# Moving part of the sums of squares at the end of the SwiGLUs to GpSimd, and spreading norm factors by fp32 products

## The chip, the cores and the metric

The kernel runs on one core of a Trainium2 chip. The metric is the device time of one execution in microseconds (us), as the median of several runs. Engines are named as in the profile: PE (TensorE, matrix products; PEld are its weight loads), DVE (VectorE), ACT (ScalarE), POOL (GpSimd), SP (SyncE, which issues DMAs). SBUF is the on-chip memory, PSUM the banks into which PE writes.

## What is computed

One inference step of a trunk of two layers, width 1024, for a prompt of 1024 tokens and for 8 x 4 sample tokens that share the weights. Layer 0 mixes tokens by sliding-window attention with sinks, layer 1 by a gated recurrence. What bears on the change are the norms and the SwiGLUs:

```
def rms_norm(x, g):
    y = xf * lax.rsqrt(jnp.mean(xf * xf, axis=-1, keepdims=True) + EPS)
    return (y * g.astype(jnp.float32)).astype(x.dtype)

def swiglu(h, w_in, w_out):
    g, u = jnp.split(h @ w_in, 2, axis=-1)
    return (jax.nn.silu(g) * u) @ w_out

for layer in range(DEPTH):
    x = x + mixer(rms_norm(x, ...))        # attention, then recurrence
    x = x + swiglu(rms_norm(x, ffn_norm[layer]), w_ffn_in[layer], w_ffn_out[layer])
y = rms_norm(x, final_norm)
```

The mean of a norm runs over the 1024 features of a token, so each of the five norms needs, per token, a sum of squares, a power of -1/2 of it, and a product of x with the result and with the norm's weight.

## The kernel before

**Layout.** Features lie on the 128 partitions, in 8 blocks (index m or kb), tokens along the free dimension in three column groups t = 0, 1, 2 of 384, 384 and 288 columns (the last: 256 prompt and 32 sample tokens). Every large product is made as three fp32r products of high and low parts (`mm3`, L313): high times high, high times low, low times high. A tile is split into such parts by `split`: ScalarE copies the high part (L351), VectorE subtracts it for the low one (L352). Weights are split on their way in: ScalarE copies (L84), VectorE subtracts (L88).

**Phases.** Attention, first FFN (l = 0), recurrence, second FFN (l = 1), final norm. In an FFN most of the products over pairs of hidden blocks are made in units of seven products instead of eight (`second`, `unit`); what is left goes through `h_out`, which ends the FFN.

**The end of an FFN (`h_out`).** For each t, and in it for each m of 8: six products into a PSUM bank, on VectorE the sum with x (L1029, with high priority), on ScalarE the square of the new x (L368), on VectorE the sum of the squares `acc` (L369). The square of m = 0 is written to `acc` itself (L365). The squares lie in a ring of two buffers that other temporary tiles share (tag "xs"). In the first FFN the squares of t = 2 are made only after `h_out`.

**A norm (`rms`, `spread`).** Three fp32 products of one column, blocks of `acc` times ones (L376), give the sums, one token per partition; VectorE scales and adds epsilon (L381), GpSimd raises to -1/2 (L382), VectorE takes the high part (L383, CAST) and the low part (L384). Six fp32r products, the high and low column of each of three token blocks times the identity `idr` (L395, L396), spread the factors over all partitions in a PSUM bank, from which ScalarE copies them (L402, `rs`). Then x is multiplied: in the mixers' and FFNs' norms at L428, after which `split` follows; in the final norm on VectorE at L1391 from the PSUM bank, and for two m of t = 1 and of t = 2 on GpSimd at L1389 (table `POOLED`). There are five norms in three groups, 15 passes in all.

**Order.** PE and SP execute in the order in which the code calls them; so where `rms` and `spread` stand between groups of products is written by hand, by `steps` in `second`: n0 and n1 are the norms of t = 0 and t = 1 that follow the FFN.

```
steps = [{}, {2: n0[1:2], 5: n0[3:4]}, {1: n1[1:2], 4: n1[3:4]}]
```

That is: the sum of t = 0 after m = 2 of t = 1, its spread after m = 5; those of t = 1 after m = 1 and m = 4 of t = 2. The order on VectorE, ScalarE and GpSimd is set by a scheduler, from its own costs and from priorities (`high_priority`). Each of these engines works strictly in its order.

**In attention** the lines that the prediction touches are: L706 and L707, the exponential of the sample tokens on ScalarE; L610 and L612, the prompt's; L712 to L714, the sample's division on VectorE, whose result `ss` PE transposes at L719; `pr`, the split probabilities; and L769, the sum of the attention's output with x. L428 there is the norm ahead of the first FFN.

Of the kernel before, what the change touches and what calls it, by code (L numbers as in the profile page):

```python
# [39 lines left out]
NSH = 4  # L40
POOLED = [(), (5, 7), (2, 5)]

# [210 lines left out]
class Kern:  # L253
# [103 lines left out]

    def square(self, t, kb):
        nc = self.nc
        W = WID[t]  # L360
        if t not in self.acc:
            self.acc[t] = self.gt.tile([P, WMAX], F32, name=self.nm("acc"), tag="acc", bufs=2)
            if W < WMAX:
                nc.gpsimd.memset(self.acc[t][:, W:WMAX], 0.0)
            nc.scalar.activation(self.acc[t][:, :W], self.xview(t, kb), AF.Square)  # L365
        else:
            sq = self.gt.tile([P, WMAX], F32, name=self.nm("sq"), tag="xs", bufs=2)
            nc.scalar.activation(sq[:, :W], self.xview(t, kb), AF.Square)  # L368
            nc.vector.tensor_tensor(self.acc[t][:, :W], self.acc[t][:, :W], sq[:, :W], OP.add)  # L369

    def rms(self, t):
        nc = self.nc
        mm = nc.tensor.matmul
        ps = self.bank()
        for b in range(3):
            mm(ps[:, WMAX + b:WMAX + b + 1], self.acc[t][:, b * P:(b + 1) * P], self.ones[:, 0:1], start=True, stop=True)  # L376
        del self.acc[t]
        col = self.gt.tile([P, 2, 3], F32, name=self.nm("rc"), tag="rc", bufs=2)
        hl = self.gt.tile([P, 2, 3], F32R, name=self.nm("rh"), tag="rh", bufs=2)
        with self.tc.high_priority(PRI):  # L380
            nc.vector.tensor_scalar(col[:, 0, :], ps[:, WMAX:WMAX + 3], 1.0 / D, EPS, op0=OP.mult, op1=OP.add)  # L381
            nc.gpsimd.tensor_tensor(col[:, 1, :], col[:, 0, :], self.mhalf, OP.pow)  # L382
            nc.vector.tensor_copy(hl[:, 0, :], col[:, 1, :])  # L383
            nc.vector.tensor_tensor(hl[:, 1, :], col[:, 1, :], hl[:, 0, :].bitcast(F32), OP.subtract)  # L384
        self.hl[t], self.col[t] = hl, col

    def spread(self, t, direct):
        nc = self.nc
        W = WID[t]
        mm = nc.tensor.matmul  # L390
        hl = self.hl[t]
        ps = self.bank()
        for b in range(3):
            o, n = b * P, min(P, W - b * P)
            mm(ps[:, o:o + n], hl[:, 0, b:b + 1].to_broadcast([P, P]), self.idr[:, :n], start=True, stop=False)  # L395
            mm(ps[:, o:o + n], hl[:, 1, b:b + 1].to_broadcast([P, P]), self.idr[:, :n], start=False, stop=True)  # L396
        self.rp[t] = ps
        if direct:
            self.rs[t] = ps
            return  # L400
        rs = self.gt.tile([P, WMAX], F32, name=self.nm("rs"), tag="rs", bufs=2)
        nc.scalar.activation(rs[:, :W], ps[:, :W], AF.Copy)  # L402
        self.rs[t] = rs
# [370 lines left out]
    def attn_phase(self):  # L774
# [31 lines left out]
        def head():  # L806
            nc.sync.dma_start(self.ident, self.I["ident"])
            nc.sync.dma_start(self.vec[:, KB:], self.I["vec"][:, KB:])
            nc.gpsimd.tensor_copy(self.idr, self.ident)

# [32 lines left out]
    def ffn_phase(self, l, before, after):  # L843
# [105 lines left out]
        def sums(j):  # L949
# [10 lines left out]
            if j == 3:  # L960
                self.freeall(self.xt[0] + self.xt[1])

        def reload(i):
            for t in range(NT):
                if i == 0:
                    self.xt[t] = []
                self.xt[t].append(self.act_tile([P, 4, WMAX], F32, "x"))
                nc.sync.dma_start(self.xt[t][i][0][:, :, :WID[t]], self.xd[t][:, 4 * i:4 * i + 4, :])
# [50 lines left out]
        def h_out(w0, w1, h, t, steps):  # L1019
            W = WID[t]  # L1020
            ws = (w0, w1)
            for m in range(KB):
# [7 lines left out]
                if l == 1 or t < 2:  # L1030
                    with tc.high_priority(PRI if t == 2 else 0):
                        self.square(t, m)
                for fn in steps.get(m, ()):
# [58 lines left out]
        def second():  # L1092
# [17 lines left out]
            def pin(on):  # L1110
# [4 lines left out]
                    [lambda: fetch(0, 3, 9), lambda: reload(1)], [lambda: do(1, "parts"), lambda: do(2, "load")],  # L1115
                    [lambda: pin(True)], [lambda: pin(False)]]
            items = []
# [16 lines left out]
            w = [x.w for x in M[n:]]  # L1134
            steps = [{}, {2: n0[1:2], 5: n0[3:4]}, {1: n1[1:2], 4: n1[3:4]}]
            last = [Item(lambda a, b, h, t=t: h_out(a, b, h, t, steps[t]), w + [H[t]],
# [19 lines left out]
        L += lead[6] + p[:2] + n0[4:] + [p[2]] + n1[4:]  # L1156
        if l == 0:
            L += [lambda m=m: self.square(2, m) for m in range(KB)]
        return L, leave
# [245 lines left out]
    def run(self):  # L1405
        nc, tc = self.nc, self.tc
        with tc.tile_pool(name="const", bufs=1) as cp, tc.tile_pool(name="g", bufs=1) as self.gp, \
# [6 lines left out]
            self.early = []  # L1414
            self.pinned = False
            self.xt, self.xn, self.acc, self.rs, self.q, self.att, self.hl, self.rp, self.col = {}, {}, {}, {}, {}, {}, {}, {}, {}
            self.ones = cp.tile([P, P], F32, name="ones")
# [4 lines left out]
            self.ident = cp.tile([P, P], F32, name="ident")  # L1422
            self.idr = cp.tile([P, P], F32R, name="idr")
            n2, n1, n3 = self.norm_steps(2, "ffn0"), self.norm_steps(1, "ffn1"), self.norm_steps(2, "ffn1")
# [109 lines left out]
```

## Time and profile before

| | |
|---|---|
| median of 3 runs | 2188.36 us (2187.37 to 2188.39) |
| the profiled execution | 2189.78 us |
| its span, first to last instruction | 2187.9 us |
| mean granted clock of PE in it | 0.987 |
| PE busy | 2129.7 us, 97% |
| VectorE, ScalarE, GpSimd busy | 1493.8, 1005.4, 232.8 us |
| sums of squares on VectorE (L369) | 105 x 525 ns = 55.1 us |
| factor's high and low part (L383, L384) | 15 x 169 and 15 x 158 ns |
| spread, high and low (L395, L396) | 45 x 271 and 45 x 293 ns |

The tables of the profile are read so: a line names an engine, the operation with what it writes and reads (`out<-in`, buffer numbers left out), partitions x elements, and how often; then the busy time, the mean of one, and the idle time of the engine just before it with what ended that. A timeline has the start, the time that it took and, in brackets, the idle time ahead and what ended it. A table of windows has, for each stretch, its length, the busy time of PE, PEld, DVE, ACT and POOL with the number of instructions, the granted clock of PE, the DMAs' share and GB/s. Matmuls are pipelined, so that the durations of single ones overlap.

### The profile page before, as it was taken

Reading aid. Unit: us, or ns where it says so; the run is one execution under the profiler, and the core shown is the slowest. Engines: PE = TensorE matmul, PEld = TensorE weight load, DVE = VectorE, ACT = ScalarE, POOL = GpSimd, SP = SyncE. Lnnn points to the kernel's source line nnn. Section 1 sums busy time; section 2 is a strip of 40 time slices with the busy share of each in tenths; the row PEclk is TensorE's granted clock in tenths of the full one; section 3 lists DMA queues with packets and bytes.
Section 4 is the critical chain, followed back from the end, with each engine's and each line's share of the span. In section 5 each row is a group of like instructions: output and inputs, shape, how many; then the busy total and the mean of one; then the engine's idle time right before and its main releaser. Section 6 shows DMA issues by size and latency. Waiting matters only on the chain.

```text
span 2187.9 us, 35226 instructions
## 1 busy us (share of the span) xinstructions
PE 2129.7 (97%) x13608; PEld 2104.4 (96%) x13608; DVE 1493.8 (68%) x2940; ACT 1005.4 (46%) x1835; POOL 232.8 (11%) x322
## 2 busy tenths in 40 slices
PE   9999999999999998999999989999999999989997
PEld 8899989999999998999999989999999999979997
DVE  6877787756656664666786787787666656556667
ACT  5666665434444443212268887754444444321122
POOL 1223230000000001232100000000000000112321
PEclk9999999999999999999999999999999999999998
DMA  5332434333343338765212123442343343676632
GB/s 193 101 104 79 129 110 159 112 106 132 104 160 120 118 137 321 287 226 185 93 43 64 59 80 114 153 147 77 137 135 129 107 162 129 220 295 220 221 121 80
DMA packets 131632, 310.12 MB, mean 142 GB/s; under 512 B 14152, under 2 KB 84872, under 8 KB 131464
## 3 DMA queue, kind: packets, MB, share of 16 engines
q1 hardware_dynamic: 130128, 306.95, 40.7%
q8 instruction: 107, 1.75, 0.3%
q10 hardware_dynamic: 1336, 0.92, 0.1%
q14 instruction: 61, 0.50, 0.1%
HBM read 223.15 MB, written 86.65 MB: 142 GB/s over the span
## 4 chain that ended last, share of the span: by engine, by line
PE 84%; DVE 7%; ACT 4%; DMA 3%; issue 1%; POOL 0%; SPq 0%; ACTq 0%; DVEq 0%; POOLq 0%
PE mm L313 80%; DVE w L88 1%; PE pt L633 1%; DMA o<-od 1%; ACT w L84 1%; DMA od<-hi 1%; PE s L585 1%; DVE s L603 1%; ACT s L610 1%; DVE xn L352 0%; DVE acc L369 0%; PE mm L376 0%; DVE pr L352 0%; DMA raw<-in_wz 0%; ACT g L1252 0%
## 5 line engine op out<-in xcount | busy, mean ns | idle before, releaser
L313 PE MATMUL mm<-xn,w 128*128 128x384 f32 (+1 forms) x5808 | 927.3, 317 | 10.6 <-DVE w L88 3.8
L313 PEld LDWEIGHTS mm<-xn,w 128*128 128x128 f32 x5808 | 901.5, 188 | 16.5 <-DVE w L88 4.5
L313 PE MATMUL mm<-o,w 128*128 128x384 f32 (+1 forms) x2928 | 478.4, 325 | 19.8 <-DVE x L1017 19.8
L313 PEld LDWEIGHTS mm<-o,w 128*128 128x128 f32 x2928 | 475.2, 191 | 20.9 <-DVE x L1017 20.9
L313 PE MATMUL mm<-T,w 128*128 128x384 f32 x1920 | 351.4, 338 | 0.9 <-ACT sg L986 0.9
L313 PEld LDWEIGHTS mm<-T,w 128*128 128x128 f32 x1920 | 338.8, 188 | 1.4 <-ACT sg L986 1.4
L88 DVE TENSOR_TENSOR w<-raw,w 128x1024 fp32r<-128x1024 f32 x202 | 245.3, 1222 | 111.2 <-ACT w L84 110.7
L1017 DVE TENSOR_TENSOR x<-mm,x 128x384 f32<-128x384 f32 x360 | 191.1, 534 | 141.3 <-PE mm L313 140.2
L84 ACT ACTIVATE w<-raw 128x1024 fp32r<-128x1024 f32 x204 | 215.1, 1056 | 129.4 <-PE mm L313 61.9
L135 ACT ACTIVATE w<-raw 128x1024 fp32r<-128x1024 f32 x84 | 85.3, 1053 | 328.4 <-POOL raw L159 296.2
L156 POOL TENSOR_TENSOR raw<-raw 128x256 f32<-128x256 f32 x40 | 29.6, 739 | 1191.4 <-DVE w L136 1191.4
L136 DVE TENSOR_TENSOR w<-raw,w 128x1024 fp32r<-128x1024 f32 x84 | 102.7, 1222 | 15.4 <-ACT w L135 15.4
L625 POOL TENSOR_SCALAR s<-s,sm 128x256 f32<-128x256 f32 (+1 forms) x128 | 83.9, 672 | 208.2 <-DVE sm L623 97.5
L313 PE MATMUL mm<-att,w 128*128 128x384 f32 (+1 forms) x576 | 97.1, 324 | 0.0
L313 PE MATMUL mm<-y,w 128*128 128x384 f32 (+1 forms) x576 | 93.5, 322 | 0.0
L313 PEld LDWEIGHTS mm<-att,w 128*128 128x128 f32 x576 | 91.3, 188 | 1.9
L313 PEld LDWEIGHTS mm<-y,w 128*128 128x128 f32 x576 | 92.4, 188 | 0.0
L610 ACT ACTIVATE s<-s,sm 128x256 f32<-128x256 f32 (+1 forms) x128 | 61.7, 483 | 45.8 <-DVE sm L607 45.7
L894 ACT ACTIVATE hi<-e 128x384 fp32r<-128x384 f32 x80 | 41.8, 523 | 88.6 <-DVE e L1008 33.4
L117 DVE TENSOR_TENSOR w<-raw,w 128x1024 fp32r<-128x1024 f32 x40 | 48.9, 1223 | 36.5 <-ACT w L115 36.4
L368 ACT ACTIVATE sq<-x 128x384 f32<-128x384 f32 (+1 forms) x105 | 50.9, 492 | 41.6 <-DVE x L1029 20.4
L992 DVE TENSOR_TENSOR sg<-mm,sg 128x384 f32<-128x384 f32 x40 | 22.2, 555 | 62.0 <-PE mm L313 62.0
(208 smaller groups left out, 2286.9 us busy)
## 6 DMA issues: line engine op xcount, KB each, us to landing
o<-od SPq DMA_DIRECT2D x70, 768.0 KB, 7.0
od<-hi SPq DMA_DIRECT2D x140, 192.0 KB, 2.0
raw<-in_wg SPq DMA_DIRECT2D x44, 512.0 KB, 4.0
raw<-in_wu SPq DMA_DIRECT2D x44, 512.0 KB, 4.5
raw<-in_wz SPq DMA_DIRECT2D x40, 512.0 KB, 3.7
od<-e SPq DMA_DIRECT2D x80, 192.0 KB, 2.0
raw<-in_wq SPq DMA_DIRECT2D x24, 512.0 KB, 3.5
raw<-in_wo SPq DMA_DIRECT2D x24, 512.0 KB, 3.6
```

Source lines behind the costliest of these rows:

```text
L84: nc.scalar.activation(self.t[:, 0, :], raw, AF.Copy)
L88: nc.vector.tensor_tensor(self.t[:, 1, :], raw, self.t[:, 0, :].bitcast(F32), OP.subtract)
L117: tt(d[:, 1, :], g, d[:, 0, :].bitcast(F32), OP.subtract)
L135: pin(nc.scalar.activation(self.t[:, 0, :], raw, AF.Copy))
L136: pin(nc.vector.tensor_tensor(self.t[:, 1, :], raw, self.t[:, 0, :].bitcast(F32), OP.subtract))
L156: tt(d, c, d, OP.add)
L313: mm = lambda *a, **k: self.nc.tensor.matmul(*a, skip_group_check=more, **k)
L368: nc.scalar.activation(sq[:, :W], self.xview(t, kb), AF.Square)
L610: nc.scalar.activation(s[:, j, :N], s[:, j, :N], AF.Exp, bias=sm[:, 1, j:j + 1], accum_out=sm[:, 3, j:j + 1])
L625: nc.gpsimd.tensor_scalar(s[:, j, :N], s[:, j, :N], sm[:, 4, j:j + 1], 1.0, op0=OP.mult, op1=OP.mult)
L894: nc.scalar.activation(hi.bitcast(F32R), src, AF.Copy)
L1017: tc.keep_in_program_order(tt(x, ps[:, :WID[t]], x, OP.add))
```

## The change

1. `square` can send its add to GpSimd. A table `SQUARES` says which: in the first FFN the squares 1 to 7 of t = 0; in the second those, 4 to 6 of t = 1, and 1 to 4 of t = 2. That is 21 of the 105 adds.
2. The squares of `h_out` lie in a ring of four buffers in a free activation slot, which the ring takes ahead of `h_out` and, in the first FFN, gives back before the squares of t = 2.
3. A spread is three fp32 products with the fp32 identity instead of six fp32r ones. The high and low parts of the factor (L383, L384) go, and `idr` with the cast that made it.
4. The sum and spread of t = 1 stand after m = 3 and 6 of t = 2 in the first FFN, after m = 2 and 5 in the second (before: 1 and 4 in both).
5. In the final norm GpSimd multiplies m = 3 and 7 of t = 1 instead of 5 and 7.

```
-POOLED = [(), (5, 7), (2, 5)]
+POOLED = [(), (3, 7), (2, 5)]
+SQUARES = [["vggggggg", "vvvvvvvv"], ["vggggggg", "vvvvgggv", "vggggvvv"]]
...
-    def square(self, t, kb):
+    def square(self, t, kb, to="v"):
...
-            sq = self.gt.tile([P, WMAX], F32, name=self.nm("sq"), tag="xs", bufs=2)
+            if self.ring:
+                sq = self.ring[0]
+                self.ring = self.ring[1:] + [sq]
+            else:
+                sq = self.gt.tile([P, WMAX], F32, name=self.nm("sq"), tag="xs", bufs=2)
             nc.scalar.activation(sq[:, :W], self.xview(t, kb), AF.Square)
-            nc.vector.tensor_tensor(self.acc[t][:, :W], self.acc[t][:, :W], sq[:, :W], OP.add)
+            e = nc.gpsimd if to == "g" else nc.vector
+            e.tensor_tensor(self.acc[t][:, :W], self.acc[t][:, :W], sq[:, :W], OP.add)
...
             nc.gpsimd.tensor_tensor(col[:, 1, :], col[:, 0, :], self.mhalf, OP.pow)
-            nc.vector.tensor_copy(hl[:, 0, :], col[:, 1, :])
-            nc.vector.tensor_tensor(hl[:, 1, :], col[:, 1, :], hl[:, 0, :].bitcast(F32), OP.subtract)
...
-            mm(ps[:, o:o + n], hl[:, 0, b:b + 1].to_broadcast([P, P]), self.idr[:, :n], start=True, stop=False)
-            mm(ps[:, o:o + n], hl[:, 1, b:b + 1].to_broadcast([P, P]), self.idr[:, :n], start=False, stop=True)
+            mm(ps[:, o:o + n], self.col[t][:, 1, b:b + 1].to_broadcast([P, P]), self.ident[:, :n], start=True, stop=True)
...
+        def ring():
+            T["ring"] = [self.act_tile([P, 4, WMAX], F32, "sq")]
+            self.ring = [T["ring"][0][0][:, k] for k in range(4)]
...
-                        self.square(t, m)
+                        self.square(t, m, SQUARES[l][t][m])
...
-                    [lambda: pin(True)], [lambda: pin(False)]]
+                    [lambda: pin(True)], [lambda: pin(False), ring]]
...
-            steps = [{}, {2: n0[1:2], 5: n0[3:4]}, {1: n1[1:2], 4: n1[3:4]}]
+            steps = [{}, {2: n0[1:2], 5: n0[3:4]}, {2: n1[1:2], 5: n1[3:4]} if l else {3: n1[1:2], 6: n1[3:4]}]
```

The line numbers shift: L369 becomes L376, L376 becomes L383, L382 becomes L388, L395 and L396 become L398, L402 becomes L404, L1029 becomes L1038, L1391 becomes L1401, L1389 becomes L1399, L428 becomes L430, L313 becomes L314.

**What moves, at three places.** VectorE, end of the second FFN, around the norm of t = 1. The names: `acc_21805` is the sum of t = 1, `acc_21923` that of t = 2, `x_19386` the x of t = 2, `x_19382` the x of t = 0, which the final norm multiplies. Before:

```order
L1029 TENSOR_TENSOR x_19386<-mm_21915,x_19386 128x288
L369 TENSOR_TENSOR acc_21805<-acc_21805,sq_21889 128x384
L1029 TENSOR_TENSOR x_19386<-mm_21926,x_19386 128x288
L369 TENSOR_TENSOR acc_21805<-acc_21805,sq_21900 128x384
L1391 SCALAR_TENSOR_TENSOR x_19382<-x_19382,vec,mm_21872 128x384
L369 TENSOR_TENSOR acc_21923<-acc_21923,sq_21934 128x288
L381 TENSOR_SCALAR rc_21941<-mm_21937 128x3
```

The same place now, where `acc_21712` is the sum of t = 1, `x_19299` the x of t = 2 and `x_19295` that of t = 0:

```order
L1038 TENSOR_TENSOR x_19299<-mm_21809,x_19299 128x288
L1401 SCALAR_TENSOR_TENSOR x_19295<-x_19295,vec,mm_21771 128x384
L1038 TENSOR_TENSOR x_19299<-mm_21820,x_19299 128x288
L1038 TENSOR_TENSOR x_19299<-mm_21830,x_19299 128x288
L376 TENSOR_TENSOR acc_21712<-acc_21712,sq_21623 128x384
L1401 SCALAR_TENSOR_TENSOR x_19295<-x_19295,vec,mm_21771 128x384
L387 TENSOR_SCALAR rc_21844<-mm_21840 128x3
```

The last sum of t = 1 now stands behind the adds to x of three groups of t = 2 instead of two, and no sum of t = 2 is left near it.

GpSimd, end of the second FFN, now. `acc_21632`, `acc_21712` and `acc_21817` are the sums of t = 0, 1 and 2, `rc` the factors of the norms; before, the two powers stood here with the MEMSET alone:

```order
L376 TENSOR_TENSOR acc_21632<-acc_21632,sq_21623 128x384 x7
L366 MEMSET acc_21817 128x96
L388 TENSOR_TENSOR rc_21738<-rc_21738,mhalf 128x3
L376 TENSOR_TENSOR acc_21712<-acc_21712,sq_21623 128x384 x3
L376 TENSOR_TENSOR acc_21817<-acc_21817,sq_21623 128x288 x2
L388 TENSOR_TENSOR rc_21844<-rc_21844,mhalf 128x3
L376 TENSOR_TENSOR acc_21817<-acc_21817,sq_21623 128x288 x2
```

The power of t = 0 now stands behind seven adds, that of t = 1 behind five more.

VectorE, third round of attention, ahead of PE's transposes of `ss` (here `ss_3911`, with its sums `sm_3912`; `pr_3931` and `pr_3939` are the prompt's probabilities). Before:

```order
L352 TENSOR_TENSOR pr_3931<-pt_3926,pr_3931 128x512
L352 TENSOR_TENSOR pr_3939<-pt_3934,pr_3939 128x512
L352 TENSOR_TENSOR xn_4103<-x_1991,xn_4103 128x384
L428 SCALAR_TENSOR_TENSOR x_1992<-x_1992,vec,rs_3750 128x384
L622 TENSOR_TENSOR sm_3957<-sm_3957 128x4
L428 SCALAR_TENSOR_TENSOR x_1992<-x_1992,vec,rs_3750 128x384
L712 TENSOR_TENSOR sm_3912<-sm_3912 128x1
L623 RECIPROCAL sm_3957<-sm_3957 128x4
L352 TENSOR_TENSOR att_3883<-mm_3997,att_3883 128x2x128
L713 RECIPROCAL sm_3912<-sm_3912 128x1
L352 TENSOR_TENSOR xn_4103<-x_1991,xn_4103 128x384
L714 TENSOR_SCALAR ss_3911<-ss_3911,sm_3912 128x264
```

Now, where `ss_3885` and `sm_3886` are the same tiles:

```order
L353 TENSOR_TENSOR pr_3905<-pt_3900,pr_3905 128x512
L608 TENSOR_SCALAR sm_3931<-sm_3931 128x4
L609 TENSOR_TENSOR sm_3931<-sink,sm_3931 128x4
L741 COPY as_98<-mm_3962 64x8x8 x2
L714 TENSOR_TENSOR sm_3886<-sm_3886 128x1
L353 TENSOR_TENSOR pr_3913<-pt_3908,pr_3913 128x512
L715 RECIPROCAL sm_3886<-sm_3886 128x1
L353 TENSOR_TENSOR xn_4077<-x_1971,xn_4077 128x384
L716 TENSOR_SCALAR ss_3885<-ss_3885,sm_3886 128x264
```

The sample's division comes ahead of two products of the norm (L430), of the prompt's sums and of the split of `att`. On PE the number of products falls by 45; on SP nothing moves.

More of the change, by code (lines that the diff above doesn't have):

```diff
@@ L378, in rms @@
         col = self.gt.tile([P, 2, 3], F32, name=self.nm("rc"), tag="rc", bufs=2)
-        hl = self.gt.tile([P, 2, 3], F32R, name=self.nm("rh"), tag="rh", bufs=2)
         with self.tc.high_priority(PRI):
@@ L382, in rms @@
             nc.gpsimd.tensor_tensor(col[:, 1, :], col[:, 0, :], self.mhalf, OP.pow)
-            nc.vector.tensor_copy(hl[:, 0, :], col[:, 1, :])
-            nc.vector.tensor_tensor(hl[:, 1, :], col[:, 1, :], hl[:, 0, :].bitcast(F32), OP.subtract)
-        self.hl[t], self.col[t] = hl, col
+        self.col[t] = col
     def spread(self, t, direct):
@@ L390, in spread @@
         mm = nc.tensor.matmul
-        hl = self.hl[t]
         ps = self.bank()
@@ L808, in head @@
             nc.sync.dma_start(self.vec[:, KB:], self.I["vec"][:, KB:])
-            nc.gpsimd.tensor_copy(self.idr, self.ident)
         def warm():
@@ L961, in sums, with unring @@
                 self.freeall(self.xt[0] + self.xt[1])
+        def ring():
+            T["ring"] = [self.act_tile([P, 4, WMAX], F32, "sq")]
+            self.ring = [T["ring"][0][0][:, k] for k in range(4)]
+        def unring():
+            self.ring = []
+            self.freeall(T["ring"])
         def reload(i):
@@ L1157, in ffn_phase @@
         if l == 0:
+            L += [unring]
             L += [lambda m=m: self.square(2, m) for m in range(KB)]
@@ L1415, in run @@
             self.pinned = False
+            self.ring = []
             self.xt, self.xn, self.acc, self.rs, self.q, self.att, self.hl, self.rp, self.col = {}, {}, {}, {}, {}, {}, {}, {}, {}
@@ L1422, in run @@
             self.ident = cp.tile([P, P], F32, name="ident")
-            self.idr = cp.tile([P, P], F32R, name="idr")
             n2, n1, n3 = self.norm_steps(2, "ffn0"), self.norm_steps(1, "ffn1"), self.norm_steps(2, "ffn1")
```

## The prediction

> **What bounds the kernel now.** The page first: how busy the engines are, and which carries the chain of work that ended last.
>
> ```profile
> PE 2129.7 (97%) x13608; PEld 2104.4 (96%) x13608; DVE 1493.8 (68%) x2940; ACT 1005.4 (46%) x1835; POOL 232.8 (11%) x322
> PE 84%; DVE 7%; ACT 4%; DMA 3%; issue 1%; POOL 0%; SPq 0%; ACTq 0%; DVEq 0%; POOLq 0%
> ```
>
> PE is the bound. A change can only shorten what PE waits, what PE does, the stretches in which its clock is halved, and what follows its last product. So I read PE's waits next (columns: total, times, longest).
>
> ```profile
> PE mm L376 <- DVE acc L369: 6.7, 3, 3.6
> PE mm L313 <- DVE x L769: 1.8, 1, 1.8
> PE mm L719 <- DVE ss L714: 2.1, 1, 2.1
> PE mm L395 <- DVE rh L383: 1.4, 1, 1.4
> ```
>
> The first and the last lie in code that the diff edits: PE waits until VectorE has added the last square, and until it has cast the norm's factor. The other two lie in attention and at the start of the first FFN, where only VectorE's order changes. That is at most 6.7+1.4+1.8+2.1 = 12.0 us, and the half clock that such waits are followed by. The timeline of the end of the second FFN (start, duration, in brackets the idle time before):
>
> ```profile
> 2164.66 0.83 PE L376 MATMUL mm<-ones,acc 128*128 128x1 f32 x6 [1.80 <-DVE acc L369]
> 2169.97 2.60 PE L313 MATMUL mm<-o,w 128*128 128x288 f32 x18
> 2170.95 2.19 POOL L1389 TENSOR_TENSOR x<-x,rs 128x384 f32<-128x384 f32 x2 [4.32 <-ACT rs L402]
> 2171.34 0.93 DVE L369 TENSOR_TENSOR acc<-acc,sq 128x288 f32<-128x288 f32 x1
> 2174.72 0.45 DVE L1029 TENSOR_TENSOR x<-mm,x 128x288 f32<-128x288 f32 x1
> 2176.18 1.44 PE L376 MATMUL mm<-ones,acc 128*128 128x1 f32 x6 [3.61 <-DVE acc L369]
> 2177.97 0.85 POOL L382 TENSOR_TENSOR rc<-rc,mhalf 128x3 f32<-128x3 f32 x1 [4.83 <-DVE rc L381]
> 2178.85 0.17 DVE L383 CAST rh<-rc 128x3 fp32r<-128x3 f32 x1 [0.51 <-POOL rc L382]
> 2179.07 0.47 PE L395 MATMUL mm<-idr,rh 128*128 128x128 f32 x1 [1.45 <-DVE rh L383]
> 2180.14 0.41 PE L396 MATMUL mm<-idr,rh 128*128 128x128 f32 x1
> 2180.53 0.37 PE L396 MATMUL mm<-idr,rh 128*128 128x32 f32 x1
> 2181.43 1.54 POOL L1389 TENSOR_TENSOR x<-x,rs 128x288 f32<-128x288 f32 x2 [2.62 <-ACT rs L402]
> ```
>
> The last group of products is over at 2169.97+2.60 = 2172.57, yet its add to x starts at 2174.72: 2.15 us in VectorE's queue. The granted clock by windows (the column after the five engines):
>
> ```profile
> 2165.50:2168.90 3.40, 3.40 (x15) 3.40 (x16) 1.98 (x8) 0.98 (x2) 0.85 (x1) 0.50 0.00 0
> 2176.00:2180.00 4.00, 2.26 (x9) 1.99 (x9) 2.48 (x8) 0.00 (x0) 0.85 (x1) 0.50 0.30 122
> ```
>
> After the wait of 1.80 us the clock stands at 0.50 for 3.4 us with PE busy throughout, which costs 1.7 us of work.
>
> **The change part by part.**
>
> *1. End of the second FFN.*
> (a) The norm of t1 is read one group later. A group lasts 2.60/3 = 0.87 us here. But VectorE's last add for t1 now stands behind the adds to x of three t2 groups, so PE still waits for an add to x and the add of a square behind it: 0.45 + about 0.55 us, some 1.05. GpSimd may by then have begun its first t2 add. VectorE's add of 2171.34 took 0.93 us beside GpSimd's L1389, against 0.45 for the 288-wide add to x, which reads PSUM. So up to 0.8 us (half of the 1.54 at 2181.43) comes on top: the wait is 1.05 to 1.85, I take 1.5. Gain 0.3. The halved window costs 1.7 and is then a toss-up; I take half, 0.85.
> (b) The norm of t2: VectorE has three adds of squares left where it had seven, so the last add to x and the last square come earlier. From the end of the products: one factor product under way (0.6, as L428's below), the add to x (0.45), another factor product and the add of the square make 2.1 us if nothing is blocked, 3.1 if each of GpSimd's two L1389 holds a step up by the 0.48 seen at 2171.34. I take 2.6 against 3.61: gain 1.0.
> (c) The last factor: GpSimd's power ends at 2178.82, the last product at 2180.90. Without CAST and the low part, three products of two passes start at once; six passes at 0.2 us, the step from 2180.14 to 2180.53 being two of them, are 1.2 to 1.3 us at the halved clock. Gain 0.65 (0.5 to 0.8).
> Together 2.8 us (1 to 5). By the exclusive lock in the Trainium skill (SBUF — State Buffer, section "SBUF: two separate sides"), a VectorE instruction with two SBUF inputs blocks wholly behind a GpSimd one that began first; the 0.93 us agree, and by the rule without exception (a) would gain nothing and the sum of this part would be about 1.4.
>
> *2. GpSimd's adds.* 21 adds leave VectorE, 14 of them 384 wide for t0 (7 in each FFN), 3 for t1 and 4 of 288 for t2. Two 384-wide L1389 took 2.19 us (1.10 each, with VectorE beside them), two 288-wide ones 1.54 (0.77, so 1.03 when scaled to 384). For t0 there is this much room in the first FFN:
>
> ```profile
> 1083.23 1.22 DVE L88 TENSOR_TENSOR w<-raw,w 128x1024 fp32r<-128x1024 f32 x1
> 1092.21 0.83 PE L376 MATMUL mm<-ones,acc 128*128 128x1 f32 x6
> ```
>
> GpSimd can start when that split is over, 1084.45, and has 7.76 us for seven adds: 1.11 each. With 1.03 and about 0.08 between two it just keeps pace; at 1.22 PE waits 0.8 to 1.3 us. I take 0.3 for both FFNs together, between 0 and 2.4. The VectorE time that goes hides under PE there, and the ring's slot comes free some units of the FFN before it is asked for, so the ring costs nothing; the other two products that GpSimd does at the end, one of them now at m = 3, cost what they did.
>
> *3. The spread.* Old: six fp32r products, one record each. New: three fp32 products. The groups and a window of the only fp32 products of that form:
>
> ```profile
> L376 PE MATMUL mm<-ones,acc 128*128 128x1 f32 x90 | 11.9, 247 | 6.8 <-DVE acc L369 6.7
> L395 PE MATMUL mm<-idr,rh 128*128 128x128 f32 (+1 forms) x45 | 10.9, 271 | 1.4 <-DVE rh L383 1.4
> 4.60:7.20 2.60, 2.60 (x24) 2.60 (x23) 1.00 0.96 318
> ```
>
> The 45 fp32 products of the 15 norms are 90 records, two passes each; L395's 45 records are three a norm, and L396, its low part, makes it six. The 24 records of L816 (128 columns, fp32) in 2.60 us are 0.108 us apiece, so a spread is 6 x 0.108 = 0.65 us after. As many passes as before, of the same width: I take 0; were a product one pass, each spread would gain 0.33.
> The Trainium skill (FP8 and Floating Point Precision, "TensorE Precision Notes") gives true fp32 four passes. By that a spread would be 12 passes, 1.3 us, and the 15 of them 9.7 us more; the 90 records speak for two.
>
> *4. End of the first FFN.* Timeline and clock:
>
> ```profile
> 1101.98 0.83 PE L376 MATMUL mm<-ones,acc 128*128 128x1 f32 x6 [1.31 <-DVE acc L369]
> 1109.75 4.31 PE L313 MATMUL mm<-xn,w 128*128 128x384 f32 x22
> 1114.06 0.55 DVE L352 TENSOR_TENSOR xn<-xs,xn 128x384 fp32r<-128x384 f32 x1
> 1114.66 1.50 PE L313 MATMUL mm<-xn,w 128*128 128x384 f32 x7 [0.60 <-DVE xn L352]
> 1103.97:1107.38 3.41, 3.41 (x18) 3.41 (x17) 2.99 (x9) 0.65 (x2) 0.28 (x1) 0.51 0.00 0
> ```
>
> Two groups later for t1's norm removes the 1.31 us, and with it the halved 3.41 us (1.7). So the next phase starts 3 us sooner, but its first products need the low part that VectorE finishes at 1114.61, and of VectorE's steps up to there only some three are gone or come later, at 0.55 like this one: an estimate of 1.5 us. The wait for it grows from 0.60 to about 2.1, and may halve the clock itself. Of 3 us I keep 0.7 (-0.2 to 1.5).
>
> *5. VectorE's order in attention and before the first FFN.* With the casts gone the scheduler spreads t0's norm differently.
>
> ```profile
> L610 ACT ACTIVATE s<-s,sm 128x256 f32<-128x256 f32 (+1 forms) x128 | 61.7, 483 | 45.8 <-DVE sm L607 45.7
> 314.39 2.32 PE L313 MATMUL mm<-pr,V 128*128 128x256 f32 x11 [1.12 <-DVE pr L352]
> 315.47 0.50 ACT L707 ACTIVATE ss<-ss,sm 128x264 f32<-128x264 f32 x1
> 318.14 0.57 DVE L714 TENSOR_SCALAR ss<-ss,sm 128x264 f32<-128x264 f32 x1
> 318.86 0.45 PE L719 MATMUL mm<-ident,ss 128*128 128x128 f32 x1 [2.15 <-DVE ss L714]
> 315.49:322.32 6.83, 4.68 (x26) 3.10 (x24) 4.81 (x15) 3.04 (x9) 2.56 (x4) 0.50 0.20 75
> ```
>
> L707 stood behind the prompt's four softmax steps L610 on ScalarE, and now comes ahead of them: 4 x 0.483 = 1.93 us, which puts L714's end at 316.8. Of the VectorE steps that go behind it I count one, like the 0.61 of L428 below: 316.2. PE gets there at 316.7: 2.15 gained, about 0.2 of the 1.12 too, and the 4.68 us of PE work at half clock (2.3 lost) I count half. 3.5 us, 0 to 5: the lower end if VectorE makes PE wait elsewhere.
>
> ```profile
> 384.51 0.61 DVE L428 SCALAR_TENSOR_TENSOR x<-x,vec,rs 128x384 f32<-128x384 f32 x1
> 385.04 0.45 DVE L769 TENSOR_TENSOR x<-mm,x 128x288 f32<-128x288 f32 x1
> 385.63 5.99 PE L313 MATMUL mm<-xn,w 128*128 128x384 f32 x24 [1.81 <-DVE x L769]
> 387.17:390.58 3.41, 3.41 (x13) 3.41 (x12) 3.41 (x8) 1.23 (x3) 0.00 (x0) 0.51 1.03 324
> ```
>
> Here the add to x no longer stands behind the norm product of 384.51: 0.53 us, and the halved window (1.7) may go. 1.2 us (0 to 2.2).
>
> **The sum.** 2.8 - 0.3 + 0 + 0.7 + 3.5 + 1.2 = 7.9 us. The profiled execution took 2189.78 us (span 2187.9), so it would take 2181.9; it stood 1.42 above the median of 2188.36, so the median would be 2180.5. All parts at their better ends give 13.7 us, at the worse ones (and GpSimd's 2.4) 1.4 us lost.
>
> **The rivals.**
> - *The gains are given back* (0.18). PE leaves attention sooner and waits for VectorE at the next place, and the first FFN's end brings nothing: only part 1 and a little of 5 are left, 3 to 4 us, 2184.5 to 2185. For it: VectorE is busy 4.81 of the 6.83 us from 315.49, and has as much to do as before. Against it: that leaves 2.0 us, about the stall that goes.
> - *GpSimd's add too slow: slower than before* (0.06). VectorE's add doubled from 0.45 to 0.93 beside GpSimd; if each GpSimd add is held up as much, 1.03+0.48 and 0.08 make 1.6 us, seven of them 11.2, and PE waits 3.4 us at t0's norm in each FFN, each with a halved window of 1.7. That is 10.2 us; with the 8.2 of the other parts and without part 5's 4.7 it ends at 2188.36 - 3.5 + 10.2 = 2195.1. It outweighs the gain of the other parts (8.2) from about 1.45 us per add on, gap included. Against it: in t0's stretch VectorE only adds PSUM to x but for one or two splits.
> - *fp32 in four passes* (0.04): 2180.5 + 9.7 = 2190.2, no change to speak of. Against it: the 90 records.
>
> **The chances.** About 0.2%, 4.4 us, can be told from no change; faster thus means below 2184.0. My forecast has 0.72, of which 0.70 falls below that. Given back: 0.04 faster, 0.14 the same. Too slow: 0.06 slower. Four passes: the same. In all 0.74, 0.20, 0.06. The range leaves out the tail of both sides: 2175, all parts near their better ends, to 2187.5.
>
> **What would show it.** In the changed profile: waits at the three one-column products in the second FFN of 0, about 1.5 and 2.6 us; GpSimd's 384-wide adds near 1.03 to 1.1; six records a spread, 0.11 apart; no wait for ss near 316 and full clock in part of 315 to 322; a wait for the low part near 1110 of about 2 us. I am wrong if GpSimd's adds take over 1.2 us, if 15 spreads show 180 records, or if the attention stretch ends no sooner than before.

## The result, and the profile after

The changed kernel takes 2177.27 us (median of 4 runs, 2174.34 to 2178.62), the kernel before 2187.9 us (4 runs, 2187.37 to 2188.39). The ratio is 0.9944, 95% interval 0.9932 to 0.9956: 12 us faster by the ratio, 10.6 by the medians. The forecast was 2180.5 us with a range of 2175 to 2187.5. The profiled execution after is the fastest of the four, 2174.34 us with a span of 2171.3; so the differences between the two traces add up to 16.6 us, more than the medians show, and are read by place, not as a total.

The engines' line of the page, after:

```profile
PE 2117.0 (97%) x13608; PEld 2093.8 (96%) x13608; DVE 1480.6 (68%) x2889; ACT 1005.4 (46%) x1835; POOL 253.4 (12%) x342
```

PE has as many records as before and 12.7 us less busy time: it is not only that waits went. PE's waits, after (total, times, longest):

```profile
PE mm L314 <- DVE w L89: 5.9, 5, 2.3
PE mm L383 <- DVE acc L376: 4.2, 2, 3.2
PE mm L721 <- DVE ss L716: 1.2, 1, 1.2
PE mm L398 <- POOL rc L388: 1.2, 1, 1.2
PE mm L314 <- DVE x L771: 1.0, 1, 1.0
```

The waits for the last squares fell from 6.7 to 4.2 us, that for ss from 2.1 to 1.2 (another place, near 335), those for x from 1.8 to 1.0. The wait for the factor stays, now for GpSimd's power itself.

The third round of attention in the timeline after, and its window:

```profile
315.13 1.21 PE L314 MATMUL mm<-pr,V 128*128 128x256 f32 x8 [0.79 <-DVE pr L353]
315.52 0.35 DVE L716 TENSOR_SCALAR ss<-ss,sm 128x264 f32<-128x264 f32 x1
316.18 0.27 PE L721 MATMUL mm<-ident,ss 128*128 128x128 f32 x1
```

```profile
315.49:322.32 6.83, 6.83 (x57) 5.88 (x56) 6.32 (x26) 3.65 (x12) 1.85 (x4) 1.00 0.23 79
```

L716 ends at 315.87, PE's transpose follows at once, and the stretch that was halved before is at full clock with PE busy throughout. At the start of the first FFN:

```profile
379.45 4.40 PE L314 MATMUL mm<-xn,w 128*128 128x384 f32 x24 [0.97 <-DVE x L771]
```

The same 24 products took 5.99 us before. At the end of the first FFN, and in its window:

```profile
1092.10 0.72 PE L383 MATMUL mm<-ones,acc 128*128 128x1 f32 x6
1096.60 2.50 PE L314 MATMUL mm<-xn,w 128*128 128x384 f32 x13
1099.46 1.14 PE L314 MATMUL mm<-xn,w 128*128 128x384 f32 x5 [0.36 <-DVE xn L353]
1102.59 3.75 PE L314 MATMUL mm<-xn,w 128*128 128x384 f32 x11 [1.14 <-DVE xn L353]
```

```profile
1102.79:1106.20 3.41, 3.41 (x12) 3.41 (x13) 2.28 (x8) 1.62 (x4) 0.00 (x0) 0.52 0.50 154
```

The wait ahead of the sum is gone, but it comes back at the next phase's products, here with a half clock behind it. The end of the second FFN:

```profile
2133.39 7.63 POOL L376 TENSOR_TENSOR acc<-acc,sq 128x384 f32<-128x384 f32 x7 [25.07 <-ACT sq L374]
2141.48 0.72 PE L383 MATMUL mm<-ones,acc 128*128 128x1 f32 x6
2151.05 0.55 DVE L376 TENSOR_TENSOR acc<-acc,sq 128x384 f32<-128x384 f32 x1
2151.05 2.09 POOL L376 TENSOR_TENSOR acc<-acc,sq 128x288 f32<-128x288 f32 x2 [1.20 <-ACT sq L374]
2151.65 0.83 PE L383 MATMUL mm<-ones,acc 128*128 128x1 f32 x6 [1.02 <-DVE acc L376]
2154.56 1.69 POOL L376 TENSOR_TENSOR acc<-acc,sq 128x288 f32<-128x288 f32 x2 [0.60 <-ACT sq L374]
2156.46 2.11 POOL L1399 TENSOR_TENSOR x<-x,rs 128x384 f32<-128x384 f32 x2 [0.21 <-ACT rs L404]
2157.68 1.20 DVE L376 TENSOR_TENSOR acc<-acc,sq 128x288 f32<-128x288 f32 x1
2160.42 1.10 PE L383 MATMUL mm<-ones,acc 128*128 128x1 f32 x6 [3.20 <-DVE acc L376]
2162.72 1.49 PE L398 MATMUL mm<-ident,rc 128*128 128x128 f32 x6 [1.19 <-POOL rc L388]
```

```profile
2152.40:2155.80 3.40, 3.40 (x28) 3.40 (x28) 2.82 (x7) 1.13 (x3) 2.72 (x4) 1.00 0.45 183
```

Seven of GpSimd's adds take 7.63 us, 1.09 each, and PE's sum of t = 0 does not wait. The sum of t = 1 waits 1.02 us and leaves the clock at 1.00. The last sum still waits 3.20.

**Where the time went, by place.** Both traces hold the same large products in the same order. The table takes the start of the same product in both and shows by how much a stretch became longer or shorter than in the profile before (us; the last column is the difference of the spans).

| kernel | attention 302-352 | start of FFN 1 352-411 | FFN 1 411-1099 | its end 1099-1121 | 1441-1465 | 1465-2150 | end 2150- | whole |
|---|---|---|---|---|---|---|---|---|
| changed | -5.0 | -2.4 | -2.2 | 0.0 | +1.7 | -4.1 | -3.6 | -16.6 |
| e1_spread_only | -5.0 | -2.4 | -2.1 | -1.0 | +1.7 | -3.0 | -0.7 | -12.6 |
| e2_old_spread | -0.4 | 0.0 | +0.3 | 0.0 | 0.0 | +0.6 | -2.0 | -1.4 |
| e3_steps_only | -2.0 | 0.0 | 0.0 | +2.8 | +0.9 | +0.4 | -1.3 | +1.4 |
| e4_all_vector | -5.0 | -2.4 | -2.8 | 0.0 | +1.7 | -3.0 | -0.4 | -12.4 |
| e5_old_steps | -3.7 | -2.5 | -1.8 | -1.3 | +1.7 | -3.4 | -3.7 | -14.4 |
| e6_idr_kept | -5.0 | -2.5 | -2.9 | 0.0 | +1.7 | -2.3 | -3.3 | -14.9 |
| x2_hi_only | -5.2 | -0.4 | +0.4 | +1.0 | +3.8 | -1.0 | +0.2 | -2.5 |
| x4_twice | -0.2 | -0.9 | -2.2 | -1.8 | +1.8 | -2.5 | -2.1 | -6.3 |
| e10_gpsimd_all | -5.1 | -2.4 | -1.7 | -2.0 | +1.7 | -2.0 | -3.4 | -15.0 |
| e12_after_pad | -5.0 | -2.4 | -0.8 | -1.6 | +3.3 | +0.9 | -3.3 | -9.1 |
| e13_before_pad | -0.2 | 0.0 | -3.3 | +0.3 | +0.4 | -3.1 | -1.3 | -6.3 |
| e14_best | -3.4 | -2.5 | -0.9 | -1.3 | +3.3 | -3.1 | -5.0 | -13.1 |

(Here and below "FFN 1" is the first one. The stretches left out changed by up to 1.0 us, in x4 by 1.6.) Two executions differ by 1 to 2 us in a stretch with waits: e3 shows -2.0 in attention though VectorE's order there is that of before, row for row. So single cells carry their sign only from about 2 us on, or where several kernels agree.

### The profile page after: what moved, and what is told of

The parts are those of the page before. It is cut to its first block, busy times and chain, and to the rows that moved or that the text cites. A ratio compares the mean times of both kernels' runs of the same rounds, so it can differ in the third digit from the quotient of the medians.

```text
span 2171.3 us, 35218 instructions
## 1 busy us (share of the span) xinstructions
PE 2117.0 (97%) x13608; PEld 2093.8 (96%) x13608; DVE 1480.6 (68%) x2889; ACT 1005.4 (46%) x1835; POOL 253.4 (12%) x342
## 4 chain that ended last, share of the span: by engine, by line
PE 85%; DVE 6%; ACT 4%; DMA 3%; issue 1%; POOL 1%; SPq 0%; DVEq 0%; ACTq 0%; POOLq 0%
PE mm L314 81%; DMA o<-od 1%; ACT w L85 1%; DVE w L89 1%; PE pt L635 1%; PE s L587 1%; DVE s L605 1%; ACT s L612 1%; DMA od<-hi 1%; DMA raw<-in_wz 0%; DVE xn L353 0%; ACT g L1262 0%; PE mm L383 0%; DVE g L1310 0%; DVE pr L353 0%
## 5 line engine op out<-in xcount | busy, mean ns | idle before, releaser
L314 PE MATMUL mm<-xn,w 128*128 128x384 f32 (+1 forms) x5808 | 928.7, 318 | 12.3 <-DVE w L89 5.2
L314 PEld LDWEIGHTS mm<-xn,w 128*128 128x128 f32 x5808 | 903.2, 188 | 18.0 <-DVE w L89 6.3
L314 PE MATMUL mm<-o,w 128*128 128x384 f32 (+1 forms) x2928 | 474.0, 323 | 19.7 <-DVE x L1026 19.7
L314 PEld LDWEIGHTS mm<-o,w 128*128 128x128 f32 x2928 | 470.6, 189 | 20.8 <-DVE x L1026 20.8
L314 PE MATMUL mm<-T,w 128*128 128x384 f32 x1920 | 347.1, 336 | 0.1
L314 PEld LDWEIGHTS mm<-T,w 128*128 128x128 f32 x1920 | 334.8, 188 | 0.5 <-ACT e L999 0.4
L314 PE MATMUL mm<-att,w 128*128 128x384 f32 (+1 forms) x576 | 97.3, 325 | 0.0
L314 PEld LDWEIGHTS mm<-att,w 128*128 128x128 f32 x576 | 91.4, 188 | 1.9
L314 PE MATMUL mm<-y,w 128*128 128x384 f32 (+1 forms) x576 | 93.1, 322 | 0.0
L314 PEld LDWEIGHTS mm<-y,w 128*128 128x128 f32 x576 | 91.9, 188 | 0.0
```

Of the source, the lines that this page charges most:

```text
L314: mm = lambda *a, **k: self.nc.tensor.matmul(*a, skip_group_check=more, **k)
```

## The experiments

Times are medians; the ratio is to the kernel before on the same chip.

### Which part of the change: e1 to e4

e1 is the kernel before with the new spread alone:

```
-            mm(..., hl[:, 0, b:b + 1].to_broadcast([P, P]), self.idr[:, :n], start=True, stop=False)
-            mm(..., hl[:, 1, b:b + 1].to_broadcast([P, P]), self.idr[:, :n], start=False, stop=True)
+            mm(..., self.col[t][:, 1, b:b + 1].to_broadcast([P, P]), self.ident[:, :n], start=True, stop=True)
```

> The kernel before with the fp32 spread alone (no casts, no idr); sums, steps and ring as before. Theory A (the larger part of the gain is VectorE's new order in attention and at the start of the first FFN, which comes from the casts being gone): 6 to 9 us faster than before, no wait for ss near 316, the end of the second FFN as before but for 0.6 us after the last power. Theory B (the gain comes from the ends of the FFNs, from GpSimd's adds and the later norm of t = 1): at most 2 us faster. Theory C (products in the FFN's units run at a slightly shorter pitch because tiles lie at other addresses once idr is gone): the products of the first FFN's units take 353.3 us as in the changed kernel's profile, not 354.7 as before.

Measured: 2179.62 us, ratio 0.9953 (0.9941 to 0.9966), so 10.3 us faster (7.4 to 12.9): nearly the whole change, somewhat more than A expected, and far from B. Its attention and its start of the FFN gained what the changed kernel's did. The 2,220 products that are PE's records 3,281 to 5,500, which lie in the first FFN's units, took 353.29 us from the first start to the last one, against 354.73 before, as C has it.

e2 is the changed kernel with the old spread, casts and idr:

> The changed kernel with the old spread (casts and six fp32r products back): GpSimd's adds, ring and later norm of t = 1 remain. A: 2 to 4 us faster than before, the wait of 2.15 us for ss in attention is back. B: 8 us or more faster. C: the units of the first FFN take 354.7 us again.

Measured: 2187.21 us, ratio 0.9988 (0.9979 to 0.9996), 2.6 us faster. A again, at its lower end. Two of PE's waits in e2:

```profile
PE mm L725 <- DVE ss L720: 2.2, 1, 2.2
PE mm L314 <- DVE x L775: 1.8, 1, 1.8
```

Both are back to the size before. The 2,220 products took 354.73 us.

e3 is the kernel before with the later sum and spread of t = 1:

```
-            steps = [{}, {2: n0[1:2], 5: n0[3:4]}, {1: n1[1:2], 4: n1[3:4]}]
+            steps = [{}, {2: n0[1:2], 5: n0[3:4]}, {2: n1[1:2], 5: n1[3:4]} if l else {3: n1[1:2], 6: n1[3:4]}]
```

> The kernel before with the later sum and spread of t = 1 alone. A and B: 0 to 1.5 us faster; the wait of 1.31 us at the end of the first FFN goes but comes back as a wait for the first products of the next phase, the wait of 1.80 us near the end falls to about 1, the one of 3.61 us stays or grows, since all sums are still VectorE's.

Measured: 2189.0 us, ratio 0.9998 (0.9989 to 1.0007): no difference. In the table the end of the first FFN is 2.8 us longer than before and that of the second 1.3 shorter.

e4 is the changed kernel with every square added on VectorE:

```
-SQUARES = [["vggggggg", "vvvvvvvv"], ["vggggggg", "vvvvgggv", "vggggvvv"]]
+SQUARES = [["vvvvvvvv", "vvvvvvvv"], ["vvvvvvvv", "vvvvvvvv", "vvvvvvvv"]]
```

> The changed kernel with all 21 sums back on VectorE (ring, fp32 spread and later norm of t = 1 remain). A: 2 to 3 us slower than the changed kernel, all of it at the end of the second FFN, where the wait for the last sum is 3.6 us or more and that for t = 1 is 1 to 2 us; 8 to 9 us faster than before. B: most of the gain gone, within 3 us of before.

Measured: 2179.23 us, ratio 0.9951 (0.9939 to 0.9964), about 10.7 us faster than before and 1.5 slower than the changed kernel by the ratios (their intervals overlap); in the traces the end is 3.1 us longer. The waits for t = 1 and t = 2 there, and VectorE's last products in e4 and in the changed kernel:

```profile
2152.72 0.83 PE L383 MATMUL mm<-ones,acc 128*128 128x1 f32 x6 [1.01 <-DVE acc L376]
2161.98 1.41 PE L383 MATMUL mm<-ones,acc 128*128 128x1 f32 x6 [3.69 <-DVE acc L376]
2166.62 2.64 DVE L1401 SCALAR_TENSOR_TENSOR x<-x,vec,mm 128x288 f32<-128x288 f32 x6 [0.33 <-ACT rs L404]
```

```profile
2164.69 2.64 DVE L1401 SCALAR_TENSOR_TENSOR x<-x,vec,mm 128x288 f32<-128x288 f32 x6 [0.87 <-ACT rs L404]
```

The last wait grows from 3.20 to 3.69 us without GpSimd's adds, but this is a small part of the 3.1 us: 2.3 of them lie behind VectorE's last product, which is over 6.2 us ahead of the end in e4 and 4.0 in the changed kernel, while the output is written. The wait for t = 1 is as short as in the changed kernel. That is not the later place alone: with the old place it is 1.13 us in e1 and 1.11 in e5, and with the later place alone, in e3, 1.01; either the new spread or the later place is enough.

### Where the sum of t = 1 stands: e5

The changed kernel with the old table of steps (the diff of e3, reversed).

> The changed kernel with the sum and spread of t = 1 back after m = 1 and 4 of t = 2. If the later place is worth what it was counted at (about 1 us in both ends): 0.5 to 2 us slower than the changed kernel, the wait of 1.3 us at the end of the first FFN is back and that for the next phase's first products is shorter by as much; the end of the second FFN waits 2 us or more for t = 1. Rival (the place decides much): 3 us or more slower.

Measured: 2174.81 us, ratio 0.9937 (0.9922 to 0.9952): not slower than the changed kernel, and the expectation fails. The wait of 1.14 us ahead of the sum is back at the first FFN's end, yet that stretch is 1.3 us shorter than in the changed kernel; at the second FFN's end both are equal, and t = 1 waits 1.11 us where 2 or more were expected:

```profile
2153.24 0.83 PE L383 MATMUL mm<-ones,acc 128*128 128x1 f32 x6 [1.11 <-DVE acc L376]
```

So no gain of the later place shows. That the old one is better is not shown either: what e5 lacks at the first FFN's end is the halved window. In e12 (below), whose VectorE and ScalarE have the changed kernel's order throughout, the same wait of 1.14 us left the clock at 1.00, and the stretch is 1.6 us shorter as well:

```profile
1103.42 8.77 PE L314 MATMUL mm<-xn,w 128*128 128x384 f32 x49 [1.14 <-DVE xn L353]
1103.42:1106.83 3.41, 3.41 (x20) 3.41 (x21) 3.10 (x9) 1.88 (x4) 0.00 (x0) 1.00 0.48 154
```

### What sets VectorE's order: x2 and x4

Casts aside, the order on VectorE up to the first FFN is the same, row for row, in the changed kernel and in e1, e4, e5 and e6, and that of before in e2 and e3. Two more kernels tell the casts and the number of products apart. x2 leaves casts and idr in the kernel before, and makes three fp32r products of the high part only:

```
-            mm(..., hl[:, 0, b:b + 1].to_broadcast([P, P]), self.idr[:, :n], start=True, stop=False)
-            mm(..., hl[:, 1, b:b + 1].to_broadcast([P, P]), self.idr[:, :n], start=False, stop=True)
+            mm(..., hl[:, 0, b:b + 1].to_broadcast([P, P]), self.idr[:, :n], start=True, stop=True)
```

> The kernel before with three fp32r products a spread, the high part alone (the low part of the norm's factor is left out); the casts, idr and VectorE's work stay. VectorE's order in attention is then that of the changed kernel. If the order alone is the cause there (and not the VectorE time or the wait for the casts): no wait for ss near 316, full clock from 315 to 322, and attention and the start of the first FFN gain 6 to 7 us as in the run with the spread alone; besides three passes of 0.11 us go from each spread, 5 us in all. 10 to 13 us faster than before. Rival (the casts on VectorE are what delays attention): at most 6 us faster, with the wait for ss still there.

Measured: 2185.86 us, ratio 0.9985 (0.9976 to 0.9994), 3.3 us faster: far below the 10 to 13, and within the rival's 6. VectorE's order, casts aside, is that of the changed kernel, row for row, almost to the end of the first FFN. And attention went as the first theory says, 5.2 us shorter and without the wait for ss at that place, so the rival's cause is out. The start of the FFN did not:

```profile
379.54 5.97 PE L313 MATMUL mm<-xn,w 128*128 128x384 f32 x24 [2.15 <-DVE x L768]
```

VectorE delivers this x at 379.40, as in the changed kernel (379.30). PE came there 1.1 us sooner with its shorter spreads, waited so much longer, and then ran at half clock. Later places took the rest of the passes back (1441 to 1465: +3.8 us). What PE saves ahead of a place where VectorE ends last was no gain here.

x4 is the changed kernel with each of the three products made twice:

```
+            for _ in range(2):
-            mm(ps[:, o:o + n], self.col[t][:, 1, b:b + 1]...)
+                mm(ps[:, o:o + n], self.col[t][:, 1, b:b + 1]...)
```

> The changed kernel with each of the three fp32 products of a spread made twice. VectorE's order in attention is then again that of the kernel before, though no cast is back. If order is the cause: the wait of about 2 us for ss and the half clock behind it are back, the 6 to 7 us of attention and the start of the FFN are lost, and 15 spreads at 6 more passes of 0.108 us cost 9.7 us: 14 to 17 us slower than the changed kernel. Rival (VectorE freed of casts is the cause): only the passes, 8 to 10 us slower than the changed kernel. By four passes a product (Trainium skill): 15 x 12 x 0.108 = 19 us for the doubled products alone, and 360 records of the spread; by two, 180.

Measured: 2184.56 us, ratio 0.9981 (0.9972 to 0.999), 8 us slower than the changed kernel by the ratios (0.9981 against 0.9944): below the expected 14 to 17 and, as a number, what the rival expected. The trace speaks against the rival: VectorE's order is that of before, row for row, up to 398 us, the wait for ss is back, and attention's gain of 5 us is gone, without a cast on VectorE:

```profile
320.96 0.45 PE L722 MATMUL mm<-ident,ss 128*128 128x128 f32 x1 [2.20 <-DVE ss L717]
```

What fell short is the price of the added products, for which 9.7 us were expected. Outside attention and the start of the first FFN the trace of x4 is only 3.9 us longer than that of the changed kernel: PE works longer, but it waits about 2 us less there, and 3.4 us of half clock at 1102 and 3.4 of the 6.8 us near 1290 that the changed kernel has did not come. The groups of the spread in the changed kernel, then in x4:

```profile
L398 PE MATMUL mm<-ident,rc 128*128 128x128 f32 (+1 forms) x90 | 12.8, 280 | 1.2 <-POOL rc L388 1.2
```

```profile
L399 PE MATMUL mm<-ident,rc 128*128 128x128 f32 (+1 forms) x180 | 23.4, 282 | 1.2 <-POOL rc L388 1.2
```

45 products are 90 records and 90 are 180: two records each, with the spread's mean of 280 ns a record against 271 and 293 before.

So the order follows the number of products that the scheduler counts in a spread: three of either type give the new order, six of either type the old one, whether VectorE casts or not.

### What sets the products' pitch: e6, e12, e13

e6 keeps the unread tile idr (64 KB in all, 512 bytes a partition) and its cast in the changed kernel.

> The changed kernel with the tile idr and the cast that fills it kept, though nothing reads it; VectorE's order is that of the changed kernel. C (addresses set the pitch of the products): the units of the first FFN take 354.7 us instead of 353.3, and the whole is about 4 us slower than the changed kernel. Rival (the pitch follows from the spread itself): 353.3 us stays, no change in time.

Measured: 2177.55 us, ratio 0.9951 (0.9939 to 0.9964), and 353.29 us for the 2,220 products: idr is not the cause. But the fast pitch went with another tile: all kernels without the two small tiles of the factor's parts (changed, e1, e4, e5, e6) had 353.29 us, all with them (before, e2, e3) 354.73. In the built programs these tiles take 64 bytes a partition, and every pool behind them moves by as much: the FFN's weight tiles start at byte 193,920 before (0 modulo 128) and at 193,344 after (64 modulo 128). e12 and e13 add an idle tile of 64 bytes to the changed kernel and to the kernel before:

```
+            nc.gpsimd.memset(self.gt.tile([P, 16], F32, name="pad", tag="pad", bufs=1), 0.0)
```

> The changed kernel with an idle tile of 64 bytes a partition (one MEMSET at the start, nothing reads it) in the pool from which the change took the two small tiles of the factor's parts. It puts the FFNs' weight tiles, which the change moved to addresses of 64 modulo 128, back to 0 modulo 128; VectorE's order stays that of the changed kernel. Theory C, now with these tiles in place of idr: the units of the first FFN take 354.7 us instead of 353.3, and the whole is 4 to 5 us slower than the changed kernel. Rival (the fp32 products of the spread set the pitch): 353.3 us stays and the time is that of the changed kernel.

Measured for e12: 2180.73 us, ratio 0.9964 (0.9952 to 0.9977): 4.4 us slower than the changed kernel by the ratios (their intervals just overlap), and 354.73 us for the 2,220 products.

> The kernel before with the same idle tile of 64 bytes, which moves its FFNs' weight tiles from 0 to 64 modulo 128; its instructions and their order stay, but for one MEMSET. Theory C: the units of the first FFN take 353.3 us, the whole is 4 to 5 us faster than before. Rival: 354.7 us, no change.

Measured for e13: 2182.03 us, ratio 0.9965 (0.9951 to 0.9978): 7.7 us faster than before (4.8 to 10.7) by one idle tile, and 352.45 us for the 2,220 products. The group of the FFN's first products (x1920) in the page of before, of the changed kernel, of e12 and of e13, with busy time and mean:

```profile
L313 PE MATMUL mm<-T,w 128*128 128x384 f32 x1920 | 351.4, 338 | 0.9 <-ACT sg L986 0.9
```

```profile
L314 PE MATMUL mm<-T,w 128*128 128x384 f32 x1920 | 347.1, 336 | 0.1
```

```profile
L314 PE MATMUL mm<-T,w 128*128 128x384 f32 x1920 | 351.4, 338 | 0.6 <-ACT sg L995 0.6
```

```profile
L313 PE MATMUL mm<-T,w 128*128 128x384 f32 x1920 | 348.4, 336 | 1.2 <-ACT e L990 0.9 <-ACT sg L986 0.2
```

The mean goes with the address, not with the kernel; and on VectorE and ScalarE e12 has the order of the changed kernel and e13 that of before, row for row, to the end. That the addresses of the pools behind the tile are the cause is shown; which of the tiles in them it is (the weights are one), why PE runs 0.4% faster from 64 modulo 128, and any other offset was not tried.

### More work on GpSimd: e10 and e14

e10 gives GpSimd all squares but the first of each group ("vggggggg" five times).

> The changed kernel with all squares but the first of each group added on GpSimd, in both FFNs. If GpSimd keeps pace (1.09 us a 384-wide add against 1.05 us of products): for t = 1 it is at most 1 us late, PE waits 0.5 to 1.5 us more for t = 1 and 1 us less for t = 2; within 2 us of the changed kernel. Rival of the prediction (its adds are held up beside VectorE): adds of 1.4 us or more, waits of 3 us and more, 4 us or more slower than the changed kernel.

Measured: 2173.45 us, ratio 0.9928 (0.9914 to 0.9941). GpSimd's group and PE's two waits at the end:

```profile
L376 POOL TENSOR_TENSOR acc<-acc,sq 128x384 f32<-128x384 f32 (+1 forms) x35 | 34.6, 987 | 53.3 <-ACT sq L374 51.6
```

```profile
2152.48 0.83 PE L383 MATMUL mm<-ones,acc 128*128 128x1 f32 x6 [0.46 <-POOL acc L376]
2161.59 1.44 PE L383 MATMUL mm<-ones,acc 128*128 128x1 f32 x6 [3.54 <-POOL acc L376]
```

The adds stay near 1 us and the wait for t = 1 falls to 0.46; the last wait grows to 3.54, since t = 2's adds stand behind GpSimd's two products of the final norm. The rival with slow adds is refuted for this kernel.

e14 is the changed kernel with the old steps, t = 2's squares all on GpSimd, and t = 1's products of the final norm all on VectorE:

> The changed kernel with the sum and spread of t = 1 after m = 1 and 4 of t = 2 again, all of t = 2's adds in the second FFN on GpSimd, and GpSimd's two products of the final norm for t = 1 on VectorE. If the old place is better at the first FFN's end (1.3 us) and VectorE's adds behind GpSimd's products are what delays the last sum (3.2 us of wait): the last wait falls to about 2 us, and the kernel is 1.5 to 3 us faster than the changed one. If GpSimd's adds of 0.85 us each then end last: the wait stays near 3 us and the gain is 1.3 us or less.

Measured: 2176.73 us, ratio 0.9935 (0.9921 to 0.9949); one of its five executions took 5338 us, which nothing here explains. The last wait fell as expected. The old steps alone leave it at 3.00 (e5), so it is one of the other two edits or both:

```profile
2164.44 0.83 PE L383 MATMUL mm<-ones,acc 128*128 128x1 f32 x6 [2.21 <-POOL acc L376]
```

Its end is 5.0 us shorter than before, against 3.6 in the changed kernel. In the whole that cannot be told from e5, e10 or the changed kernel: all four intervals overlap. e10 has the lowest median; that it beats the changed kernel is not shown.

## Why the prediction was right, step by step

The sign and the range held; the sum of 7.9 us was 12 by the ratio. (The worse ends of all parts add up to 1.6 us lost, not 1.4.) Point by point:

- **Part 5, attention and the start of the first FFN: right place, too small, wrong reason.** 5.0 and 2.4 us instead of 3.5 and 1.2. L716's end was put at 316.2 and came at 315.87. The half clock was counted at half, and in the changed kernel both halved windows went. That was in part luck: in e5 and e14, with the same order on VectorE and the same wait of 0.79 us for `pr` near 315, a window of 3.4 us at half clock stayed, and attention gained 3.7 and 3.4. The reason given, the casts that are gone, fell with x2 and x4: the scheduler sees three products instead of six, though PE has six records a spread before and after.
- **Part 3, the spread: right.** Two records a product, no change on PE: from a spread's first product to the next large one 0.62 us passed before (at 1451) and 0.59 after (at 1456). The price of four passes did not come. How often the array is passed within a record these times do not tell, since records of one column (L383) come 0.11 us apart too.
- **Part 4, end of the first FFN: mechanism right, size off.** 0.0 instead of 0.7. PE did start 3 us sooner and gave all of it back: waits of 0.36, 0.42 and 1.14 us, near the 2.1 forecast, and a halved window behind them, which the prediction named as possible. Without this window, in e12, the same order gained 1.6.
- **Part 1, end of the second FFN: 3.6 instead of 2.8, in other shares.** Up to the end of the last group of products 2.3 us were gained where (a) had 1.15, behind it 1.3 where (b) and (c) had 1.65. (a) The wait for t = 1 was taken at 1.5 and is 1.02. VectorE was not held up: its add took 0.55, and GpSimd's pair that began with it 2.09, where its next pair, with no add of a square on VectorE beside it, took 1.69. The halved window, taken as a toss-up, did not come. It was one: in e13, with the order of before and the same wait (1.82 us against 1.80), it did not come either (lines below). (b) The last wait was taken at 2.6 and is 3.20, just above the upper bound of 3.1: VectorE's add took 1.20 beside GpSimd's L1399. (c) The CAST and the low part are gone, and the wait for the factor fell from 1.45 to 1.19. The 1.4 us that the prediction gives for this part under the lock does not follow from its terms: without (a), 1.65 are left.

```profile
2159.76 0.83 PE L376 MATMUL mm<-ones,acc 128*128 128x1 f32 x6 [1.82 <-DVE acc L369]
2160.00:2164.00 4.00, 4.00 (x34) 4.00 (x34) 3.23 (x11) 1.57 (x4) 0.85 (x1) 1.00 0.15 60
```

- **Part 2, GpSimd's adds: right.** 1.09 us each where 1.03 and 0.08 between two were forecast; no wait for t = 0, so the 0.3 us was not needed.
- **What the sum did not hold.** The pitch of the products (about 4.4 us by e12 against the changed kernel), from tiles that the change took away and that the prediction never looked at. And a new wait for a weight at the start of the second FFN, about 1.5 us in every kernel with the new order (2.29 in x2; 0.93 in x4, which has the old one); its cause stays open:

```profile
1452.37 1.82 PE L314 MATMUL mm<-xn,w 128*128 128x384 f32 x9 [1.47 <-DVE w L89]
```

Without the moved addresses, in e12, the change gains 7.9 us (5.0 to 10.5), the figure of the sum; but by terms that were too small and a loss that was not foreseen, so the agreement is partly luck.

The rival "given back" came true at one place, the first FFN's end, and not in attention. Neither slow adds nor the price of four passes came.

## What to carry to other kernels

A change at the end of a phase can earn most of its time elsewhere: compare the order of every engine, and read each place where it moves in the trace of before. Ask what ends last behind a wait before counting it as gained; time that PE gained here ahead of a place bound by VectorE came back as a wait, at times with a halved window behind it. Compare several traces before reading such a window as an effect of the change. When tiles are added or taken away, compare the product's pitch as well as its waits, and try the kernel before with an idle tile of the same size.

## What the runs showed of the hardware

- An idle tile of 64 bytes a partition changed PE's pitch by 0.4 to 0.6%: 354.73 us for 2,220 products with weight tiles at 0 modulo 128, 353.29 and 352.45 us at 64 modulo 128.
- Waits of 0.97 and 1.02 us left the clock at 1.00 (changed kernel, at 379 and 2151); waits of 1.81 and 2.15 us at the start of the first FFN were followed by a half clock (before, x2). But the length of the wait alone does not decide: 1.80 and 1.82 us ahead of the same sum were followed by 3.4 us at half clock before and by none in e13, 1.14 us by one in the changed kernel and by none in e12, and 1.47 us (at 1452) by none in the changed kernel and by one in e12.
- VectorE's add of a square took 0.46 us alone at 288 columns, 0.93 and 1.20 beside GpSimd's L1389 or L1399 that had begun first; begun together with GpSimd's add it took its usual 0.55 at 384 columns, and GpSimd's two 288-wide adds took 2.09 instead of the next pair's 1.69. The exclusive lock in the Trainium skill (SBUF — State Buffer, section "Who interferes with whom") fits: one of the two runs its usual time and the other is held up, the one that began later where they did not begin together.
